# Decoder blocks on one core: GpSimd taken out of the splits, token mix shared with ACT, decay by exponentials, a sixth split slot

## The chip, the cores and the metric

One core of one Trainium2 chip runs one program. The metric is the device time of one execution in microseconds; lower is better. Engines are called as in the profile: PE is TensorE, DVE VectorE, ACT ScalarE, POOL GpSimd, SP the sync engine whose queue issues the DMAs.

## The reference

Two stacked models in float32 on 256 tokens of width 1024. The first block runs three mixers side by side (differential attention, an RWKV-7 recurrence, attention over 256 memory rows), projects them back, and runs a mixture of experts with 16 experts of which two are chosen per token. Then come four SwiGLU blocks (ffn0 to ffn3, inner width 2816), a hybrid attention layer (hyb) behind ffn0 and a sliding-window one (swa) behind ffn2. The change touches above all this part:

```python
cols = cols + (prev - cols) * mu
...
w = -jax.nn.softplus(-(w0 + jnp.tanh(xw) @ w2)) - 0.5
...
decay = jnp.exp(-jnp.exp(w))
...
state = (state * w_t[:, :, None, :]
         + sa[..., None] * (kk_t * a_t)[:, :, None, :]
         + v_t[..., None] * k_t[:, :, None, :])
```

## The kernel before

**Split products.** A float32 product is done as three matmuls of a faster type (`mm3`, lines 97 to 101): every operand is split into a high half (a cast by ACT, line 93) and a low half (operand minus high half, line 94), and high x high, low x high and high x low are added in PSUM. Weights arrive by SP in 2 MB tiles ("raw", `load`, line 85) and are split 1024 columns at a time into "wh" and "wl". These go round in slots: three of the pool wsp, and from the first ffn on two more of the pool lend (`weights`, line 168; NW = 3, NV = 2). A split waits until TensorE has done with the slot's last user. `self.lo` names the engine of line 94: DVE, except for seven of the eight tiles of the recurrence's input and the K projection of the differential attention, eleven splits in all, where it is POOL. The activations are split in `prep` (lines 116 to 137): eight transposes by TensorE for each half of the tokens, in two groups a = 0, 1; for each, DVE multiplies by the gain ("xf", line 133), ACT casts to "xh" (line 134), and "xl" is taken on POOL for a = 0 and on DVE for a = 1 (line 135). `prep` runs eight times: for x, for mem, and at each of the six block boundaries. The norm's "rstd" (lines 105, 106) is on POOL.

**Boundaries.** `project_back` does its last few k tiles (TAIL) for token half 0 and then for half 1. Behind each half the sum is added to h (lines 369, 371), and `prep` of the next block runs for that half while TensorE does the other.

**The front.** `mixers` interleaves one generator, `rwkv`, with the projections. `rwkv_inputs` (from line 640) makes eight tiles: a product, "cur" = product x norm (line 653), "shd" = previous token minus this one (line 655), "mix" = shd x mu + cur (line 656), all on DVE. `rwkv` takes the decay from a sigmoid by two tanh on ACT (lines 692, 693), then on DVE 1 - z, a reciprocal and 2z - 1 (lines 709 to 711), a running product over each chunk of 64 tokens by a scan with resets (line 712), and its reciprocal (line 715).

**The MoE.** Behind the logits, h is split once more, "hx" on ACT and "hy" on POOL (lines 1170, 1171), and multiplied with one-hot places to gather the tokens of each expert. The experts' weights (100 MB) pass through slots: wsp, lend, raw and "half" tiles.

**Order.** Every engine works through its queue in order. The queues' orders are made when the program is built, by the Tile scheduler from its own estimate of a timeline (`schedule_with_timeline_sim=True`); nothing is written out by hand but the order of `staggered` and of the generators.

Of the kernel before, what the change touches and what calls it, by code (L numbers as in the profile page):

```python
# [26 lines left out]
class Net:  # L27
    def __init__(self, ctx, tc, I):
        self.ctx, self.tc, self.nc, self.I = ctx, tc, tc.nc, I
        nc = self.nc  # L30
        self.const = ctx.enter_context(tc.tile_pool(name="const", bufs=1))
        self.wk = ctx.enter_context(tc.tile_pool(name="wk", bufs=2))
        self.dram = ctx.enter_context(tc.tile_pool(name="dram", bufs=1, space=DRAM))
        self.raw0 = ctx.enter_context(tc.tile_pool(name="raw0", bufs=RAW))
        self.base = [self.raw0] * RAW
        self.wsp = ctx.enter_context(tc.tile_pool(name="wsp", bufs=NW))
        self.lend = ctx.enter_context(tc.tile_pool(name="lend", bufs=NV))
        self.ahead, self.lo, self.nsc = [], nc.vector, 3
        self.n = 0
        self.setup()  # L40
# [23 lines left out]
    def setup(self):  # L64
        nc = self.nc
        self.ident = self.const.tile([128, 128], F32, name="ident")
        nc.gpsimd.memset(self.ident, 1.0)
        nc.gpsimd.affine_select(self.ident, self.ident, pattern=[[-1, 128]], compare_op=OP.is_equal,
                                fill=0.0, base=0, channel_multiplier=1)
        self.mhalf = self.const.tile([128, 1], F32, name="mhalf")  # L70
        nc.gpsimd.memset(self.mhalf, -0.5)
        self.cols = self.const.tile([128, NCOL], F32, name="cols")
        nc.scalar.dma_start(self.cols, self.I["cols"])

    def col(self, name, i=0, n=1):
# [12 lines left out]
    def split(self, x):  # L88
        nc = self.nc
        n = x.shape[-1]  # L90
        p = next(self.splits)
        hi, lo = (p.tile([128, 1024], F32, name=self.nm(z), tag=z).bitcast(F32R) for z in ("wh", "wl"))
        nc.scalar.copy(hi[:, :n], x)  # L93
        self.lo.tensor_tensor(lo[:, :n], x, hi[:, :n].bitcast(F32), OP.subtract)  # L94
        return hi, lo
# [20 lines left out]
    def prep(self, h, gain, into=None):  # L116
# [5 lines left out]
        def fill(t):  # L122
            for a in range(2):
                ps = self.trp()
                for i in range(4):
                    k = a * 4 + i
                    nc.tensor.transpose(ps[:, i * 128:(i + 1) * 128], h[t][:, k * 128:(k + 1) * 128], self.ident)  # L127
                p3 = ps.rearrange("p (k t) -> p k t", k=4)
                dh = xh[:, a * 4:a * 4 + 4, t * 128:(t + 1) * 128]
                dl = xl[:, a * 4:a * 4 + 4, t * 128:(t + 1) * 128]  # L130
                xf = self.wk.tile([128, 4, 128], F32, name=self.nm("xf"), tag="xf")
                g = self.col(gain, a * 4, 4)
                nc.vector.tensor_tensor(xf, p3, g.unsqueeze(2).to_broadcast([128, 4, 128]), OP.mult)
                nc.scalar.copy(dh, xf)  # L134
                (nc.vector if a else nc.gpsimd).tensor_tensor(dl, xf, dh.bitcast(F32), OP.subtract)  # L135
            rs[t] = self.rms(h[t], D, 1.0 / 32)
# [25 lines left out]
    def weights(self, extra, nsplit):  # L162

        with ExitStack() as st:
            pools = list(self.base)
            if extra:
                pools += [st.enter_context(self.tc.tile_pool(name=self.nm("raw"), bufs=extra))] * extra
            self.splits = itertools.cycle([self.wsp] * NW + [self.lend] * nsplit)
            self.ring = itertools.cycle(pools)
            yield  # L170
# [261 lines left out]
    def hyb(self, h, x, follow):  # L432
# [7 lines left out]
        ps = self.projN(self.by_k(self.load(self.I["hyb_c"]), 296), 0, 296, xh, xl, True)  # L440
        cw = self.natural(ps, self.pair(264, "cw0", "cw1"), rs)
        kiT = self.repeated_T([z[:, 264:296] for z in ps], rs, "kiT", 1)
# [101 lines left out]
    def mixers(self, x, more, follow):  # L544
# [19 lines left out]
        next(rwkv)  # L564
        self.lo = nc.gpsimd
        dist, nlam = self.diff_consts()
        k = project(W[3], 512, self.lent("wl"))
        self.lo = nc.vector
        next(rwkv)
# [43 lines left out]
        self.slots = [pools[c] for c in MOE_SLOTS]  # L613
        self.lo, self.nsc = nc.vector, 4
        return logits
# [23 lines left out]
    def rwkv_inputs(self, W, xh, xl, bc):  # L639
# [3 lines left out]
        for n, i in enumerate(RW_ORDER):  # L643
# [3 lines left out]
            elif n == 4:  # L647
                raw = self.load(W[1])
            self.lo = nc.gpsimd if n else nc.vector
            ps = self.projT(self.by_col(raw, n % 4), xh, xl)  # L650
            cur = self.sb([T + 1], "cur", cls="r")
            nc.gpsimd.memset(cur[:, 0:1], 0.0)
            nc.vector.tensor_tensor(cur[:, 1:], ps[:, :T], bc, OP.mult)  # L653
            d = self.sb([T], "shd", cls="r")
            nc.vector.tensor_sub(d, cur[:, :T], cur[:, 1:])
            nc.vector.scalar_tensor_tensor(out[i // 2][:, i % 2, :], d, self.k1("mu", i, 1), cur[:, 1:],
                                           OP.mult, OP.add)
        return out

    def rwkv(self, rw):  # L660
# [10 lines left out]
        vec.tensor_scalar(half[:, 0:6], self.k1("wa0k"), 0.5, None, OP.mult)  # L671
        dk = 0.25 * math.exp(-0.5)
        vec.memset(half[:, 6:7], -dk)
        vec.memset(half[:, 7:8], -0.5)
# [15 lines left out]
        for hp in range(2):  # L690
            S = sg[:, hp, :]
            act.activation(S, zp[:, hp * T:hp * T + T], AF.Tanh, bias=half[:, hp:hp + 1], scale=0.5)
            act.activation(S, S, AF.Tanh, scale=-dk, bias=half[:, 6:7])
        for hp in range(2):
# [10 lines left out]
        for hp in range(2):  # L705
            S = sg[:, hp, :]
            dec, wx = sb([4, 65], "dec"), sb([4, 65], "wx")
            pool.memset(dec[:, :, 0:1], 0.0)
            vec.tensor_scalar(S, S, -1.0, 1.0, OP.mult, OP.add)
            vec.reciprocal(S, S)  # L710
            vec.tensor_scalar(dec[:, :, 1:], c4(S), 2.0, -1.0, OP.mult, OP.add)
            vec.tensor_tensor_scan(wx.rearrange("p c t -> p (c t)"), dec.rearrange("p c t -> p (c t)"),
                                   self.k1("reset"), 0.0, OP.mult, OP.add)
            iw = sb([4, 64], "iw")
            vec.reciprocal(iw, wx[:, :, 1:])
            Wx.append(wx)
# [414 lines left out]
    def moe(self, h, x):  # L1131
# [37 lines left out]
        for t in range(2):  # L1169
            nc.scalar.copy(hx[t], h[t])  # L1170
            nc.gpsimd.tensor_tensor(hy[t], h[t], hx[t].bitcast(F32), OP.subtract)

# [262 lines left out]
    def front(self, h):  # L1435
# [4 lines left out]
        with ExitStack() as more:  # L1440
# [3 lines left out]
            with self.phase():  # L1444
                y = self.moe(h, x)
        ahead = [self.load(self.I["ffn0"][0], 2)]
        self.moe_overflow(h)
# [65 lines left out]
for _n, _w in (("mu", 8), ("wa0k", 6), ("kk_g", 2), ("rk_g", 2), ("bsel", 2), ("wa2", 256), ("g2", 256), ("gn_w", 256),  # L1513
               ("gn_b", 256), ("maskkr", 128), ("low8", 64), ("bd8", 64), ("eye", 64), ("off16", 64), ("off32", 64),
               ("off64", 64), ("reset", 260)):
    COLS1[_n] = (NC1, _w)
# [44 lines left out]
def cols1(X):  # L1561
# [28 lines left out]
    for b in (16, 32, 64):  # L1590
        put(f"off{b}", one((q // b == m // b) & (2 * q // b != 2 * m // b)))
    put("reset", one(np.arange(260) % 65 == 0))
    return c
# [94 lines left out]
```

## Time and profile before

| | |
|---|---|
| median of 3 runs | 1452.94 us (1452.23 to 1453.97) |
| the profiled execution | 1451.34 us |
| its span in the profile | 1449.6 us, mean PE clock 0.983 |
| busy: PE, PEld, DVE, ACT, POOL | 1383.6, 1042.0, 760.6, 605.6, 127.9 us |
| HBM traffic | 291 MB read, 202 GB/s over the span |

The span goes from the first to the last instruction; the execution's own time has something around it. A group gives the busy time of all instructions of a line, engine, operation and shape, the mean of one, and the idle time of their engine just before them with what ended it. "X <- Y" in the waits reads: X stood idle until Y was done. A timeline row is one instruction or several like it (x2), in brackets its engine's idle time before it. Where a helper records the line, one line stands for many places; the tile's name tells them apart.

### The profile page before, as it was taken

What the parts mean: (1) busy time and instruction counts of PE and PEld (TensorE: products, weight loads), DVE (VectorE), ACT (ScalarE), POOL (GpSimd) and SP (SyncE); (2) the same over time, 40 slices, a digit from 0 to 9 for tenths busy, and PEclk for the clock granted to TensorE, in tenths of its full rate; (3) what the DMA queues carried; (4) which work ended last, traced back from release to release, by engine and by line L of the source; (5) the groups of instructions that cost most, each with busy time, mean ns of one, the idle gap of its engine ahead of it and who ended that gap; (6) DMA issues with size and microseconds to landing.
All of it is one profiled execution on the core that took longest, in us unless ns stands there. A gap on an engine that the chain in (4) does not pass through costs nothing.

```text
span 1449.6 us, 18902 instructions
## 1 busy us (share of the span) xinstructions
PE 1383.6 (95%) x7650; PEld 1042.0 (72%) x7650; DVE 760.6 (52%) x1233; ACT 605.6 (42%) x951; POOL 127.9 (9%) x150
## 2 busy tenths in 40 slices
PE   7899989999998999999898999999999989999997
PEld 6687664344336888878677888878888877788886
DVE  6967651112125555456865555455555466555544
ACT  5345431111114444347454444344444456444442
POOL 6514110000001000010111000010000010100001
PEclk9999889999998999999999999999999999999999
DMA  7243379999965544355333544454444632365520
GB/s 305 90 183 139 145 319 368 419 409 419 420 285 213 194 174 175 130 216 194 126 117 139 210 174 174 153 225 175 175 174 160 240 129 111 131 214 182 185 88 29
DMA packets 35371, 293.81 MB, mean 203 GB/s; under 512 B 3728, under 2 KB 8112, under 8 KB 16080
## 3 DMA queue, kind: packets, MB, share of 16 engines
q1 hardware_dynamic: 29952, 286.58, 52.4%
q10 hardware_dynamic: 5328, 5.98, 1.2%
q8 instruction: 62, 1.02, 0.3%
q14 instruction: 29, 0.24, 0.0%
HBM read 291.45 MB, written 1.10 MB: 202 GB/s over the span
## 4 chain that ended last, share of the span: by engine, by line
PE 64%; DVE 2%; ACT 1%; POOL 1%; issue 1%; ACTq 0%; POOLq 0%; DVEq 0%
PE acc L101 20%; PE acc L99 20%; PE acc L100 19%; PE tr L206 1%; PE acc L322 1%; PE tr L318 1%; DVE wl L94 1%; POOL xl L135 1%; ACT wh L93 1%; PE acc L288 1%; PE acc L289 1%; PE acc L323 0%; ACT sq L113 0%; DVE h L371 0%; PE tr L127 0%
## 5 line engine op out<-in xcount | busy, mean ns | idle before, releaser
L94 DVE TENSOR_TENSOR wl<-raw,wh 128x1024 fp32r<-128x1024 f32 (+1 forms) x338 | 412.5, 1223 | 377.6 <-ACT wh L93 377.0
L93 ACT CAST wh<-raw 128x1024 fp32r<-128x1024 f32 (+1 forms) x349 | 363.4, 1045 | 412.8 <-PE acc L101 367.7
L101 PE MATMUL acc<-wh,xl 128*128 128x512 f32 (+2 forms) x896 | 336.0, 376 | 7.2 <-POOL xl L135 7.2
L99 PE MATMUL acc<-wh,xh 128*128 128x512 f32 (+2 forms) x896 | 337.2, 378 | 1.7 <-ACT xh L134 1.2
L100 PE MATMUL acc<-wl,xh 128*128 128x512 f32 (+2 forms) x896 | 335.2, 374 | 3.0 <-DVE wl L94 3.0
L101 PEld LDWEIGHTS acc<-wh,xl 128*128 128x128 f32 x896 | 169.5, 189 | 41.4 <-POOL xl L135 9.2
L100 PEld LDWEIGHTS acc<-wl,xh 128*128 128x128 f32 x896 | 169.8, 190 | 35.3 <-DVE wl L94 3.7
L99 PEld LDWEIGHTS acc<-wh,xh 128*128 128x128 f32 x896 | 169.8, 189 | 35.1 <-ACT xh L134 2.2
L101 PE MATMUL acc<-wh,hl 128*128 128x512 f32 x352 | 137.4, 390 | 0.0
L100 PE MATMUL acc<-wl,hh 128*128 128x512 f32 x352 | 137.2, 390 | 0.0
L99 PE MATMUL acc<-wh,hh 128*128 128x512 f32 x352 | 136.7, 389 | 0.0
L105 POOL TENSOR_SCALAR rstd<-ss 128x1 f32<-128x1 f32 x22 | 8.2, 371 | 940.8 <-ACT sq L113 938.9
L101 PEld LDWEIGHTS acc<-wh,hl 128*128 128x128 f32 x352 | 66.1, 188 | 13.6
L99 PEld LDWEIGHTS acc<-wh,hh 128*128 128x128 f32 x352 | 66.1, 188 | 13.6
L100 PEld LDWEIGHTS acc<-wl,hh 128*128 128x128 f32 x352 | 66.1, 188 | 13.5
L99 PE MATMUL acc<-xh,wh 128*128 128x256 f32 x224 | 65.8, 294 | 2.1 <-DVE cur L653 1.3
L100 PE MATMUL acc<-xl,wh 128*128 128x256 f32 x224 | 63.9, 286 | 1.8 <-POOL xl L135 1.0
L101 PE MATMUL acc<-xh,wl 128*128 128x256 f32 x224 | 64.2, 288 | 0.0
L1298 PE MATMUL acc<-half,xe 128*64 128x512 f32 x248 | 59.6, 596 | 0.0
L1331 DVE TENSOR_SCALAR yf<-tr,gate 128x512 f32<-128x512 f32 x16 | 12.0, 751 | 81.0 <-PE tr L1324 80.8
L99 PEld LDWEIGHTS acc<-xh,wh 128*128 128x128 f32 x224 | 43.4, 194 | 5.9 <-ACT wh L93 2.7
L100 PEld LDWEIGHTS acc<-xl,wh 128*128 128x128 f32 x224 | 43.1, 193 | 2.5 <-POOL xl L135 1.3
(458 smaller groups left out, 1748.7 us busy)
## 6 DMA issues: line engine op xcount, KB each, us to landing
raw<-in_ffn SPq DMA_DIRECT2D x63, 2048.0 KB, 8.0
half<-in_moe SPq DMA_DIRECT2D x45, 1024.0 KB, 12.9
raw<-in_moe SPq DMA_DIRECT2D x13, 2048.0 KB, 15.6
raw<-in_hyb SPq DMA_DIRECT2D x7, 2048.0 KB, 7.9
wl<-in_moe SPq DMA_DIRECT2D x23, 512.0 KB, 13.7
wh<-in_moe SPq DMA_DIRECT2D x23, 512.0 KB, 14.8
raw<-in_win SPq DMA_DIRECT2D x4, 2048.0 KB, 10.1
raw<-in_swa SPq DMA_DIRECT2D x4, 2048.0 KB, 8.7
```

The lines of the kernel that those rows point to most:

```text
L93: nc.scalar.copy(hi[:, :n], x)
L94: self.lo.tensor_tensor(lo[:, :n], x, hi[:, :n].bitcast(F32), OP.subtract)
L99: mm(out, a[0], b[0], start=start, stop=False)
L100: mm(out, a[0], b[1], start=False, stop=False)
L101: mm(out, a[1], b[0], start=False, stop=stop)
L135: (nc.vector if a else nc.gpsimd).tensor_tensor(dl, xf, dh.bitcast(F32), OP.subtract)
L206: nc.tensor.transpose(ps[:, i * 128:(i + 1) * 128], m[:, i * 128:(i + 1) * 128], self.ident)
L288: nc.tensor.matmul(ps[:, 0:128], qT[r, 0:128], kT[r, 0:128], start=True, stop=True)
L289: nc.tensor.matmul(ps[:, 128:384], qT[r, 128:256], kT[r, :], start=True, stop=True)
L318: nc.tensor.transpose(pt[:, i * 128:(i + 1) * 128], s2[e][:, i * 128:(i + 1) * 128], self.ident)
L322: nc.tensor.matmul(po[r, :T], v[0][:, c:c + 64], pT[:, :T], start=True, stop=False)
L1298: last = mm(ps[c][e * 64:e * 64 + 64, :], xe[:, k, o + e * 64:o + e * 64 + 64], w[i][e][:, c * 512:c * 512 + 512], start=k == 0, stop=k == 7)
```

## The change

Seven things. (1) `self.lo` goes: the low half of every split is on DVE. So are "xl" for a = 0 in `prep` and "hy" in the MoE (there in four pieces of 512 columns). (2) The token mix is written as cur x (1 - mu), on ACT with a scale per partition, plus previous x mu, on DVE; a tile "keep" holds 1 - mu. (3) The decay: one tanh on ACT, + 1 on DVE, a running sum by a scan that restarts at each chunk (constant "keep" for "reset"), and two exponentials on ACT for the running product and its reciprocal. (4) `weights` opens a pool "spare" of one more slot wherever it adds lend's: six slots instead of five from ffn0 on. (5) `room` puts two unused tiles of 16 words, one in the pool of constants and one in wk. (6) A pair of tiles in hyb is 320 columns wide instead of 264. (7) The DMA scratch is 512 instead of 1024. The diff, without most of its context:

```diff
@@ -35,7 +35,7 @@
         self.lend = ctx.enter_context(tc.tile_pool(name="lend", bufs=NV))
-        self.ahead, self.lo, self.nsc = [], nc.vector, 3
+        self.ahead, self.nsc = [], 3
         self.n = 0
@@ -69,8 +69,14 @@
         nc.gpsimd.memset(self.mhalf, -0.5)
+        self.room(self.const, 16)
         self.cols = self.const.tile([128, NCOL], F32, name="cols")
         nc.scalar.dma_start(self.cols, self.I["cols"])
+
+    def room(self, pool, words):
+
+        z = pool.tile([128, words], F32, name=self.nm("room"), tag=f"room{words}", bufs=1)
+        self.nc.gpsimd.memset(z, 0.0)
@@ -91,7 +97,7 @@
         nc.scalar.copy(hi[:, :n], x)
-        self.lo.tensor_tensor(lo[:, :n], x, hi[:, :n].bitcast(F32), OP.subtract)
+        nc.vector.tensor_tensor(lo[:, :n], x, hi[:, :n].bitcast(F32), OP.subtract)
         return hi, lo
@@ -132,7 +138,7 @@
                 nc.scalar.copy(dh, xf)
-                (nc.vector if a else nc.gpsimd).tensor_tensor(dl, xf, dh.bitcast(F32), OP.subtract)
+                nc.vector.tensor_tensor(dl, xf, dh.bitcast(F32), OP.subtract)
             rs[t] = self.rms(h[t], D, 1.0 / 32)
@@ -165,7 +171,8 @@
                 pools += [st.enter_context(self.tc.tile_pool(name=self.nm("raw"), bufs=extra))] * extra
-            self.splits = itertools.cycle([self.wsp] * NW + [self.lend] * nsplit)
+            spare = [st.enter_context(self.tc.tile_pool(name=self.nm("spare"), bufs=1))] if nsplit else []
+            self.splits = itertools.cycle([self.wsp] * NW + [self.lend] * nsplit + spare)
             self.ring = itertools.cycle(pools)
@@ -438,7 +445,7 @@
         ps = self.projN(self.by_k(self.load(self.I["hyb_c"]), 296), 0, 296, xh, xl, True)
-        cw = self.natural(ps, self.pair(264, "cw0", "cw1"), rs)
+        cw = self.natural(ps, [z[:, :264] for z in self.pair(320, "cw0", "cw1")], rs)
         kiT = self.repeated_T([z[:, 264:296] for z in ps], rs, "kiT", 1)
@@ -562,10 +569,8 @@
         next(rwkv)
-        self.lo = nc.gpsimd
         dist, nlam = self.diff_consts()
         k = project(W[3], 512, self.lent("wl"))
-        self.lo = nc.vector
         next(rwkv)
@@ -611,7 +616,7 @@
         self.slots = [pools[c] for c in MOE_SLOTS]
-        self.lo, self.nsc = nc.vector, 4
+        self.nsc = 4
         return logits
@@ -646,14 +651,16 @@
                 raw = self.load(W[1])
-            self.lo = nc.gpsimd if n else nc.vector
             ps = self.projT(self.by_col(raw, n % 4), xh, xl)
...
             nc.vector.tensor_tensor(cur[:, 1:], ps[:, :T], bc, OP.mult)
+            if n == 0:
+                keep = self.sb([8], "keep", cls="r")
+                nc.vector.tensor_scalar(keep, self.k1("mu"), -1.0, 1.0, OP.mult, OP.add)
             d = self.sb([T], "shd", cls="r")
-            nc.vector.tensor_sub(d, cur[:, :T], cur[:, 1:])
-            nc.vector.scalar_tensor_tensor(out[i // 2][:, i % 2, :], d, self.k1("mu", i, 1), cur[:, 1:],
+            nc.scalar.activation(d, cur[:, 1:], AF.Copy, scale=keep[:, i:i + 1])
+            nc.vector.scalar_tensor_tensor(out[i // 2][:, i % 2, :], cur[:, :T], self.k1("mu", i, 1), d,
                                            OP.mult, OP.add)
@@ -669,8 +676,7 @@
         vec.tensor_scalar(half[:, 0:6], self.k1("wa0k"), 0.5, None, OP.mult)
-        dk = 0.25 * math.exp(-0.5)
-        vec.memset(half[:, 6:7], -dk)
+        dk = 0.5 * math.exp(-0.5)
         vec.memset(half[:, 7:8], -0.5)
@@ -690,7 +696,6 @@
             act.activation(S, zp[:, hp * T:hp * T + T], AF.Tanh, bias=half[:, hp:hp + 1], scale=0.5)
-            act.activation(S, S, AF.Tanh, scale=-dk, bias=half[:, 6:7])
         for hp in range(2):
@@ -706,13 +711,12 @@
             pool.memset(dec[:, :, 0:1], 0.0)
-            vec.tensor_scalar(S, S, -1.0, 1.0, OP.mult, OP.add)
-            vec.reciprocal(S, S)
-            vec.tensor_scalar(dec[:, :, 1:], c4(S), 2.0, -1.0, OP.mult, OP.add)
-            vec.tensor_tensor_scan(wx.rearrange("p c t -> p (c t)"), dec.rearrange("p c t -> p (c t)"),
-                                   self.k1("reset"), 0.0, OP.mult, OP.add)
+            vec.tensor_scalar(dec[:, :, 1:], c4(S), 1.0, None, OP.add)
+            vec.tensor_tensor_scan(wx.rearrange("p c t -> p (c t)"), self.k1("keep"),
+                                   dec.rearrange("p c t -> p (c t)"), 0.0, OP.mult, OP.add)
             iw = sb([4, 64], "iw")
-            vec.reciprocal(iw, wx[:, :, 1:])
+            act.activation(iw, wx[:, :, 1:], AF.Exp, scale=dk)
+            act.activation(wx, wx, AF.Exp, scale=-dk)
             Wx.append(wx)
@@ -1168,7 +1172,8 @@
             nc.scalar.copy(hx[t], h[t])
-            nc.gpsimd.tensor_tensor(hy[t], h[t], hx[t].bitcast(F32), OP.subtract)
+            for s in (slice(0, 512), slice(512, 1024)):
+                tt(hy[t][:, s], h[t][:, s], hx[t][:, s].bitcast(F32), OP.subtract)
@@ -1443,6 +1448,7 @@
                 y = self.moe(h, x)
+        self.room(self.wk, 16)
         ahead = [self.load(self.I["ffn0"][0], 2)]
@@ -1512,7 +1518,7 @@
                ("gn_b", 256), ("maskkr", 128), ("low8", 64), ("bd8", 64), ("eye", 64), ("off16", 64), ("off32", 64),
-               ("off64", 64), ("reset", 260)):
+               ("off64", 64), ("keep", 260)):
     COLS1[_n] = (NC1, _w)
@@ -1589,7 +1595,7 @@
         put(f"off{b}", one((q // b == m // b) & (2 * q // b != 2 * m // b)))
-    put("reset", one(np.arange(260) % 65 == 0))
+    put("keep", one(np.arange(260) % 65 != 0))
     return c
@@ -1677,7 +1683,7 @@
     arrays = {k: np.ascontiguousarray(v) for k, v in pack(inputs).items()}
-    nc = _bacc.Bacc("TRN2", target_bir_lowering=False, num_devices=1, dynamic_dma_scratch_size=1024)
+    nc = _bacc.Bacc("TRN2", target_bir_lowering=False, num_devices=1, dynamic_dma_scratch_size=512)
     I = {k: nc.dram_tensor(f"in_{k}", list(v.shape), mybir.dt.from_np(v.dtype), kind="ExternalInput").ap()
```

## Rows read from the trace of the kernel before

**Rows 1.** The page's busy times (part 1) and the chain that ended last (part 4).

```profile
PE 1383.6 (95%) x7650; PEld 1042.0 (72%) x7650; DVE 760.6 (52%) x1233; ACT 605.6 (42%) x951; POOL 127.9 (9%) x150
...
PE acc L101 20%; PE acc L99 20%; PE acc L100 19%; PE tr L206 1%; PE acc L322 1%; PE tr L318 1%; DVE wl L94 1%; POOL xl L135 1%; ACT wh L93 1%; PE acc L288 1%; PE acc L289 1%; PE acc L323 0%; ACT sq L113 0%; DVE h L371 0%; PE tr L127 0%
```

**Rows 2.** Whom TensorE waited for, whole span: total us, times, longest us.

```profile
PE tr L127 <- DVE xf L133: 7.8, 6, 2.4
...
PE acc L101 <- POOL xl L135: 7.2, 5, 2.2
...
PE acc L100 <- DVE wl L94: 3.0, 2, 2.4
...
PE acc L100 <- POOL xl L135: 1.0, 1, 1.0
```

**Rows 3.** Stretches: length, busy us of PE, PEld, DVE, ACT, POOL, PE clock, DMA, GB/s.

```profile
20.00:72.00 52.00, 44.44 (x309) 37.19 (x308) 48.17 (x66) 23.75 (x38) 29.87 (x25) 1.00 0.37 141
...
217.40:253.70 36.30, 36.30 (x185) 16.44 (x181) 4.85 (x13) 5.91 (x11) 0.00 (x0) 1.00 0.92 368
...
1164.50:1171.30 6.80, 5.73 (x27) 5.73 (x28) 4.05 (x4) 1.78 (x4) 2.30 (x2) 0.52 0.02 9
```

**Rows 4.** Groups of POOL: busy us, mean ns of one, idle before and its releaser.

```profile
L94 POOL TENSOR_TENSOR wl<-raw,wh 128x1024 fp32r<-128x1024 f32 x11 | 27.0, 2463 | 7.9 <-ACT wh L93 7.8
...
L135 POOL TENSOR_TENSOR xl<-xf,xh 128x512 fp32r<-128x512 f32 x14 | 21.0, 1505 | 15.1 <-ACT xh L134 15.1
...
L1171 POOL TENSOR_TENSOR hy<-h,hx 128x1024 fp32r<-128x1024 f32 x2 | 4.7, 2364 | 0.1
```

**Rows 5.** Groups of DVE, shapes apart.

```profile
L94 DVE TENSOR_TENSOR wl<-raw,wh 128x1024 fp32r<-128x1024 f32 x333 | 407.7, 1227 | 374.2 <-ACT wh L93 373.6 <-DVEq L1359 0.2
...
L656 DVE SCALAR_TENSOR_TENSOR mix<-shd,c,cur 128x256 f32<-128x256 f32 x8 | 9.7, 1217 | 0.2
...
L655 DVE TENSOR_TENSOR shd<-cur 128x256 f32<-128x256 f32 x8 | 9.5, 1187 | 0.6
...
L715 DVE RECIPROCAL iw<-wx 128x256 f32<-128x256 f32 x2 | 3.5, 1740 | 0.0
```

**Rows 6.** Timeline of the front: start, us, engine and step.

```profile
22.10 2.62 POOL L94 TENSOR_TENSOR wl<-raw,wh 128x1024 fp32r<-128x1024 f32 x1 [3.43 <-ACT wh L93]
...
22.88 2.11 DVE L655 TENSOR_TENSOR shd<-cur 128x256 f32<-128x256 f32 x1
...
25.95 0.42 DVE L655 TENSOR_TENSOR shd<-cur 128x256 f32<-128x256 f32 x1
```

**Rows 7.** Timeline of the boundary from hyb to ffn1.

```profile
773.77 1.22 DVE L94 TENSOR_TENSOR wl<-raw,wh 128x1024 fp32r<-128x1024 f32 x1
...
774.65 0.42 POOL L105 TENSOR_SCALAR rstd<-ss 128x1 f32<-128x1 f32 x1 [30.72 <-ACT sq L113]
...
776.24 1.25 PE L127 MATMUL tr<-ident,h 128*128 128x128 f32 x8 [1.54 <-DVE xf L133]
...
776.70 1.22 DVE L94 TENSOR_TENSOR wl<-raw,wh 128x1024 fp32r<-128x1024 f32 x1
...
776.92 1.08 POOL L105 TENSOR_SCALAR rstd<-ss 128x1 f32<-128x1 f32 x1 [1.20 <-ACT sq L113]
...
777.90 0.69 DVE L135 TENSOR_TENSOR xl<-xf,xh 128x512 fp32r<-128x512 f32 x1
```

**Rows 8.** Timeline of TensorE in the front, two steps behind an idle stretch.

```profile
36.91 0.35 PE L99 MATMUL acc<-xh,wh 128*128 128x256 f32 x1 [1.25 <-DVE cur L653]
...
56.71 1.26 PE L127 MATMUL tr<-ident,mem 128*128 128x128 f32 x8 [2.37 <-DVE xf L133]
```

**Rows 9.** Whom SP's DMA queue waited for, 0 to 80 us.

```profile
SPq L576 <- POOL cur L652: 14.3, 1, 14.3
```

**Rows 10.** Group of ACT in the recurrence.

```profile
L696 ACT ACTIVATE lent<-mix,c 128x256 f32<-128x256 f32 x2 | 1.0, 498 | 0.0
```

**Rows 11.** Timeline of DVE ahead of the MoE.

```profile
207.06 0.17 DVE L1229 COPY G<-rstd 128x8 f32<-128x8 f32 x1 [1.95 <-POOL rstd L106]
```

## The prediction

> **What bounds the kernel now.** I read the page's busy times and its chain first, then whom TensorE waited for, then its idle stretches in order of time with the other engines beside them. TensorE is busy 1383.6 of 1449.6 us, and the chain that ended last runs three fifths through the three matmul lines of the split product [rows 1]. So the kernel is bound by matmul work that the change doesn't touch. What an edit can win is the remaining 66.0 us of idle TensorE, and the stretches where its clock is at the lower level. The list of waits says who ends that idle time [rows 2]: "xf" on DVE 7.8 us, "xl" on POOL 7.2 and 1.0, the split's low half "wl" on DVE 3.0. The diff touches every one of these. It doesn't touch the wait behind the top-k mask in the hyb layer, nor the routing.
>
> Two places hold these waits. **The front** (20 to 72 us): DVE is busy 48.2 of 52.0 us, POOL 29.9, TensorE 44.4 [rows 3]. **The six block boundaries** (MoE to ffn0, and the five after it), where the next block's input is normalised, transposed and split while TensorE drains the last block.
>
> **Why DVE is full in the front.** POOL takes 2.46 us for a 128x1024 low half, DVE 1.22 [rows 4, 5]. While POOL does one, short DVE steps get long: the subtraction of the token mix takes 0.42 us at 25.95, but at 22.88 it takes 2.11 and ends at 24.99, as POOL's split, begun at 22.10, ends at 24.72 [rows 6]. Over the eight tiles the two mix steps cost 9.5 + 9.7 us [rows 5]; at 0.45 each, an estimate from the short one, they would cost 7.2, so some 12 us of DVE's front are this waiting. Reciprocals of 1.7 us, two for each head pair, stand in the same queue [rows 5].
>
> **The change part by part.**
>
> *Splits to DVE, front.* DVE gets 11 splits x 1.22 = 13.4 us, and four "xl" of 0.69 (attn and mem) = 2.8 [rows 5, 7]. It loses the 12 us of waiting, the eight subtractions (3.4 at 0.42), and by the decay edit four reciprocals (the two of L715 take 3.5 [rows 5], the others the same: 7). Sum: 16.2 in, about 22.4 out, so DVE's load falls by some 6 us instead of growing. TensorE's idle time there that DVE ends is 1.25 ("cur", at 36.91), 2.37 ("xf" of mem, at 56.71) [rows 8] and both waits on "wl", 3.0 [rows 2]: 6.6 us. I take **-5.5**; the rest stays because chains through DVE are still there. Bounds: -6.6, and +2 if splits queue behind each other (one and a half of them). The load of mem waited 14.3 us on SP's queue for a step of POOL's queue [rows 9], with the next weight load behind it; with the splits gone from POOL it goes out earlier, and moves with this term.
>
> *Token mix on ACT, decay by exponentials.* ACT gets eight scaled copies and four exponentials and loses two tanh, all of 256 columns, where the scaled copy that is there takes 0.50 us [rows 10]: 10 x 0.50 = +5.0 us on an engine busy 23.8 of 52.0 us [rows 3]. Taken at **0**; what hides it is TensorE's own 44 us there. If that cover were gone, one copy would be late by one high half in ACT's queue, about 1 us, on the last tile: bounds -0.5 and +1. Behind a late copy on DVE wait the mix and what follows it. The recurrence's chain loses two reciprocals and one step; what that wins is in the first term, whose last two waits stand beside it.
>
> *"xl" to DVE at the boundaries.* Here 12 of the 16 low halves leave POOL (1.51 us mean, waiting included [rows 4]) for DVE at 0.69 [rows 7], in order behind what DVE has. TensorE's waits ended by "xl" are 7.2 + 1.0 = 8.2 us, the 1.0 at the very start [rows 2]. A step that takes 0.69 for 1.51 would save 8.2 x 0.54 = 4.4; where two halves ran on both engines at once they lengthened each other, which goes too. Against it, a split (1.22) may stand in front of it. I take **-5**; bounds -8.2 and 0. Behind the new step are the "h" additions and splits, 0.69 later each; TensorE needs those only after the first k tiles.
>
> *Sixth slot.* One more slot lets one split of the next block run before the boundary. At hyb to ffn1 a split of 1.22 us stands on DVE at 773.77, in front of the addition and of "xf", for which TensorE then waits 1.54 [rows 7]. Waits on "xf" outside the front are 7.8 - 2.37 = 5.4 us [rows 2, 8]. I take **-3**, half a split at each of five; bounds -5.4 and 0. Inside a block it brings nothing, as no wait on "wl" but the front's two is in the list.
>
> *MoE "hy" to DVE.* POOL's two steps of 2.36 us [rows 4] go; DVE gets four of 0.69 (2.8 us). DVE idles 1.95 us there, waiting for a POOL "rstd" [rows 11], which covers most of it, and the logits' matmuls end no sooner: **0**, bounds -0.5 and +1.4.
>
> *Padding tiles, smaller DMA scratch, wider pair:* two memsets of 16 words, and other addresses. No row shows a time that hangs on an address: **0**, bounds -1 and +1.
>
> Sum: -5.5 - 5 - 3 = **-13.5 us**. The profiled execution took 1451.34 us, 1.7 more than its span; the median of the runs, 1452.94, is 1.6 above it. So 1437.8 for such an execution, **1439.4** against the median.
>
> One thing speaks against the change: POOL keeps the "rstd" steps, and more of DVE's work now stands beside them. At 776.92 such a step takes 1.08 us and ends at 778.00, beside a DVE split that runs from 776.70 to 777.92 [rows 7]. I add nothing for it, since the next user of "rstd" is the eviction behind all k tiles. The Trainium skill (SBUF — State Buffer, "Who interferes with whom") says that a DVE instruction with two SBUF inputs and a GpSimd one that reads SBUF shut each other out for their whole length, whichever issues first; this row agrees, and by the rule every split or "xl" moved to DVE can hold an "rstd" (a rival, below).
>
> **Rivals.**
> - *The MoE's weights eat the front's gain.* The DMA share is 0.92 at 368 GB/s in the MoE's first stretch [rows 3]; if the weights land no sooner, a TensorE that starts earlier waits. Only the boundaries count then: -8, **1445**. Against: TensorE is busy 36.3 of 36.3 us there, and the loads start on slots that the front frees.
> - *All bounds, and a clock drop with them.* -6.6 - 8.2 - 5.4, and the 6.8 us at clock 0.52 from 1164.5 [rows 3], the lower level, just behind TensorE's waits at ffn2 to swa: worth 3.3. Together -23.5: **1429**.
> - *"rstd" on POOL is late.* Lengthened from the 0.42 at 774.65 to the 1.08 at 776.92 [rows 7], at six boundaries and on the path: +4.0, **1443.4**. Against: nothing in the waits of TensorE names "rstd".
> - *Slower: DVE is the new bound.* If DVE's long steps in the front came from something else than POOL, DVE would get 16.2 us and lose 10.4: +5.8 us on an engine 93% full [rows 3], all of it on TensorE; and at five boundaries "xl" would stand behind a split, 1.22 + 0.69 against 1.51, +0.4 each. About +8: **1461**. It decides where DVE has no idle time left between 20 and 72 us. Against: the lengthened steps end with POOL's [rows 6].
> - *It doesn't do what it says:* the order on the queues is made anew, and DVE's freed time falls where TensorE doesn't wait. 0 to -2: **1452**.
>
> **Chances.** Forecast 0.56 (its own range 1433 to 1447), all bounds 0.13, DMA 0.11, "rstd" 0.05, no gain 0.07, slower 0.08. A measurement here tells about 0.2% (2.9 us) from no change. Faster by more than that: the first four, less a little of the forecast's own bounds: 0.84. Within: the fifth, 0.07. Slower: 0.09. The range runs from 1427 (all bounds, and 2 for the unknown small ones) to 1450 (short of the fifth case) and leaves out some two in ten.
>
> **What would show it.** Right: no POOL row for L94, L135 or L1171; the mix steps at 0.42 to 0.5 us; DVE under 85% busy between 20 and 72 us; the wait of L101 on "xl" under 3 us in total; the MoE's gathers 5 us sooner; a DVE split fewer between the "h" addition and "xf" at the boundaries. Wrong: DVE over 95% busy in the front, TensorE's waits on "xl" or "wl" as large as before, or new table loads on ACT in the recurrence.

## The result, and the profile after

| | before | after |
|---|---|---|
| median of 4 runs | 1453.03 us (1452.23 to 1453.97) | 1429.70 us (1428.48 to 1431.53) |
| the profiled execution, its span | 1451.34, 1449.6 us | 1430.63, 1428.9 us |
| TensorE busy / idle in the span | 1383.6 / 66.0 us | 1378.0 / 50.9 us |
| mean granted clock | 0.983 | 0.979 |

The ratio is 0.9842, 95% interval [0.9829, 0.9854]: 23.3 us faster, where 13.5 were forecast; 1429.7 lies in the range of the forecast (1427 to 1450), near its lower end. Of the 20.7 us by which the span is shorter, 15.1 are idle time of TensorE and 5.6 busy time. The forecast counted on idle time alone.

Busy times and chain of the page, which answer to [rows 1]:

```profile
PE 1378.0 (96%) x7650; PEld 1051.2 (74%) x7650; DVE 747.7 (52%) x1250; ACT 610.0 (43%) x961; POOL 77.5 (5%) x123
...
PE acc L105 20%; PE acc L107 20%; PE acc L106 20%; PE tr L213 1%; PE acc L329 1%; DVE wl L100 1%; PE tr L325 1%; PE acc L296 1%; PE acc L295 1%; PE acc L330 0%; ACT sq L119 0%; DVE h L376 0%; DVE h L378 0%; DVE xf L139 0%; ACT wh L99 0%
```

Whom TensorE waited for, against [rows 2]: the waits on GpSimd's "xl" and those on "wl" are gone, and 2.1 us of waits on "xl" from DVE are left. The wait on "xf" is 5.6 instead of 7.8. One entry is new: "ka", behind the top-k mask in hyb, 3.7 us, where the kernel before waited 6.3 us for the mask itself, "madd".

```profile
PE tr L133 <- DVE xf L139: 5.6, 5, 1.6
...
PE acc L295 <- DVE ka L386: 3.7, 2, 3.2
...
PE acc L107 <- DVE xl L141: 1.5, 2, 0.8
...
PE acc L106 <- DVE xl L141: 0.6, 1, 0.6
```

The front, as a stretch (columns as in [rows 3]), and two groups of DVE there, against [rows 5]: DVE is busy 42.1 of 52 us instead of 48.2, TensorE 50.9 instead of 44.4 (418 matmuls instead of 309), and the mix step takes 478 ns instead of 1217.

```profile
20.00:72.00 52.00, 50.89 (x418) 43.81 (x417) 42.12 (x81) 30.89 (x52) 6.25 (x14) 1.00 0.38 146
...
L100 DVE TENSOR_TENSOR wl<-raw,wh 128x1024 fp32r<-128x1024 f32 x14 | 17.1, 1220 | 5.2 <-ACT wh L99 5.2
L663 DVE SCALAR_TENSOR_TENSOR mix<-cur,c,shd 128x256 f32<-128x256 f32 x8 | 3.8, 478 | 0.3 <-POOL cur L656 0.3
```

The same 52 us hold more work now. Up to 6.5 us behind the first gather of the MoE, where both kernels have done the same 1709 matmuls, TensorE's idle time falls from 25.7 to 16.3 us and DVE's busy time from 155.7 to 141.1. Before, then after, columns as in [rows 3]:

```profile
0.00:217.40 217.40, 191.71 (x1709) 153.96 (x1711) 155.71 (x327) 96.30 (x195) 79.13 (x86) 0.95 0.51 197
```

```profile
0.00:206.90 206.90, 190.56 (x1709) 156.58 (x1711) 141.07 (x332) 100.12 (x205) 44.90 (x71) 0.94 0.53 207
```

The MoE's gathers, a tile's summary (first and last start): before, then after. The first starts 10.5 us sooner and the last 10.4, so the lead stays unchanged through the MoE.

```profile
L1189 PE MATMUL tr<-P,hx x64: 274/283/553, 210.9 to 370.7; 128*128 128x256 f32 x64
```

```profile
L1194 PE MATMUL tr<-P,hx x64: 278/283/553, 200.4 to 360.3; 128*128 128x256 f32 x64
```

Behind the MoE the lead was followed from matmul to matmul, each against the one of the same tile and number in the other trace. It is 10.5 us at the end of the MoE, 8.3 at the start of ffn0, 10.5 at its end, 12.1 in hyb, 13.2 and 15.6 at the start and end of ffn1, 15.3 and 17.6 of ffn2, 17.7 at the end of swa, 18.4 and 20.6 at the start and end of ffn3. Within each ffn it grows at an even pace over the first 120 us, by 2.7 us, gives back some 0.4 and then stands still. Boundaries do not look like that. The two rows below show a stretch of 80 us in the up half of ffn1, in which TensorE is busy throughout at the upper clock: 357 matmuls before, 370 after.

```profile
796.00:876.00 80.00, 80.00 (x357) 64.76 (x356) 43.15 (x42) 36.15 (x40) 0.00 (x0) 1.00 0.53 193
```

```profile
783.00:863.00 80.00, 80.00 (x370) 66.47 (x369) 44.81 (x44) 38.38 (x43) 0.00 (x0) 1.00 0.55 198
```

The timeline of TensorE in ffn0 shows why, before and after: nine matmuls take 2.10 us, and 2.04. From start to start the median over the kernel is 233 ns before and 227 after, in all three matmuls of a split product whose stationary operand is xh or xl. In the down half, with hh and hl, it is 227 or 226 in both kernels. (The up half of an ffn multiplies the normalised input xh, xl by the first weights, the down half the inner activations hh, hl by the last.)

```profile
500.15 0.39 PE L100 MATMUL acc<-wl,xh 128*128 128x512 f32 x1
...
502.25 0.39 PE L100 MATMUL acc<-wl,xh 128*128 128x512 f32 x1
```

```profile
490.87 0.39 PE L106 MATMUL acc<-wl,xh 128*128 128x512 f32 x1
...
492.91 0.39 PE L106 MATMUL acc<-wl,xh 128*128 128x512 f32 x1
```

The last weights of each up half are taken with 256 moving columns, and there it is the other way round. Nine matmuls take 1.02 us before and 1.08 after, 113 ns and 120 from start to start, which is what the lead gives back:

```profile
573.02 0.28 PE L99 MATMUL acc<-wh,xh 128*128 128x256 f32 x1
...
574.04 0.28 PE L99 MATMUL acc<-wh,xh 128*128 128x256 f32 x1
```

```profile
562.03 0.28 PE L105 MATMUL acc<-wh,xh 128*128 128x256 f32 x1
...
563.11 0.28 PE L105 MATMUL acc<-wh,xh 128*128 128x256 f32 x1
```

So the lead grows by 2.2 to 2.4 us in each ffn, by 9.1 in the four.

And the clock: at two levels, full and half, a mean of 0.983 is half clock in 2 x 0.017 x 1449.6 = 49 us, one of 0.979 in 60 us. Between MoE and ffn0 the lower level lasts longer (columns as in [rows 3], before and then after), which is where the lead fell from 10.5 to 8.3.

```profile
444.00:455.00 11.00, 8.14 (x27) 6.38 (x28) 9.79 (x13) 4.33 (x8) 3.24 (x6) 0.53 0.74 279
```

```profile
434.00:448.00 14.00, 10.60 (x32) 7.91 (x33) 11.64 (x17) 5.51 (x9) 2.50 (x4) 0.51 0.81 317
```

### The profile page after: what moved, and what is told of

It reads as the page before. It is cut to its first block, busy times and chain, and to the rows that moved or that the text cites. A ratio compares the mean times of both kernels' runs of the same rounds, so it can differ in the third digit from the quotient of the medians.

```text
span 1428.9 us, 18895 instructions
## 1 busy us (share of the span) xinstructions
PE 1378.0 (96%) x7650; PEld 1051.2 (74%) x7650; DVE 747.7 (52%) x1250; ACT 610.0 (43%) x961; POOL 77.5 (5%) x123
## 3 DMA queue, kind: packets, MB, share of 16 engines
q8 instruction: 62, 1.02, 0.3%
## 4 chain that ended last, share of the span: by engine, by line
PE 65%; DVE 3%; ACT 1%; issue 1%; ACTq 0%; POOLq 0%; POOL 0%
PE acc L105 20%; PE acc L107 20%; PE acc L106 20%; PE tr L213 1%; PE acc L329 1%; DVE wl L100 1%; PE tr L325 1%; PE acc L296 1%; PE acc L295 1%; PE acc L330 0%; ACT sq L119 0%; DVE h L376 0%; DVE h L378 0%; DVE xf L139 0%; ACT wh L99 0%
## 5 line engine op out<-in xcount | busy, mean ns | idle before, releaser
L100 DVE TENSOR_TENSOR wl<-raw,wh 128x1024 fp32r<-128x1024 f32 (+1 forms) x349 | 426.1, 1224 | 377.0 <-ACT wh L99 374.9
L105 PE MATMUL acc<-wh,xh 128*128 128x512 f32 (+1 forms) x896 | 334.5, 375 | 2.4 <-ACT xh L140 1.8
L106 PE MATMUL acc<-wl,xh 128*128 128x512 f32 (+1 forms) x896 | 333.1, 372 | 0.0
L105 PEld LDWEIGHTS acc<-wh,hh 128*128 128x128 f32 x352 | 66.1, 188 | 13.5
```

Of the source, the lines that this page charges most:

```text
L100: nc.vector.tensor_tensor(lo[:, :n], x, hi[:, :n].bitcast(F32), OP.subtract)
L105: mm(out, a[0], b[0], start=start, stop=False)
L106: mm(out, a[0], b[1], start=False, stop=False)
```

## Experiments

Each kernel is named by its label. The kernel before ran beside each of them; its medians there were 1451.68 to 1453.68 us.

| kernel | us | ratio to before, 95% interval | TensorE idle, us | spacing with xh, ns |
|---|---|---|---|---|
| before_pads | 1446.31 | 0.9951 [0.9932, 0.9970] | 64.1 | 227 |
| after_nopads | 1441.43 | 0.9928 [0.9912, 0.9945] | 53.6 | 233 |
| after_noc | 1428.10 | 0.9830 [0.9813, 0.9846] | 51.5 | 227 |
| after_now | 1438.04 | 0.9901 [0.9885, 0.9918] | 51.8 | 233 |
| slots5_off128 | 1435.66 | 0.9885 [0.9869, 0.9902] | 52.8 | 232 |
| before_lodve | 1445.93 | 0.9941 [0.9919, 0.9964] | 59.2 | |
| before_mixdec | 1448.26 | 0.9971 [0.9960, 0.9982] | 61.0 | |
| before_front | 1449.00 | 0.9973 [0.9957, 0.9990] | 65.5 | |
| before_front_xl2 | 1439.25 | 0.9907 [0.9892, 0.9922] | 53.8 | |
| after_xlpool | 1439.10 | 0.9909 [0.9892, 0.9925] | 60.4 | |
| after_xlbound | 1429.77 | 0.9837 [0.9823, 0.9850] | 52.4 | |
| after_5slots | 1426.23 | 0.9820 [0.9806, 0.9833] | 51.1 | |

Idle is span less TensorE's busy time, from the page; the spacing is the median from start to start of acc<-wh,xh with 512 columns.

### The addresses

**before_pads**: the kernel before with the change's addresses.

```diff
+        self.room(self.const, 16)
...
+        self.room(self.wk, 16)
...
-        cw = self.natural(ps, self.pair(264, "cw0", "cw1"), rs)
+        cw = self.natural(ps, [z[:, :264] for z in self.pair(320, "cw0", "cw1")], rs)
...
-dynamic_dma_scratch_size=1024
+dynamic_dma_scratch_size=512
```

> The kernel before with the addresses of the change alone: the two unused tiles of 16 words, the DMA scratch of 512 and the pair of 320 columns. Every queue keeps its order; only the two memsets come in. xh and xl move from 448 to 0, wh and wl from 384 to 0 (byte address in the partition, modulo 512). Theory P (the address decides how fast the matmuls of the up half of an ffn follow each other, 233 ns before and 227 after): the spacing of acc<-wh,xh falls to 227 ns, the time by 9 to 12 us, to about 1442. Rival Q (the spacing comes from another part of the change, the sixth slot or GpSimd's absence): spacing stays 233 ns, time within 1 us of before.

Spacing 227: the addresses alone do it. The time fell by 7 us by the ratio and 5.4 by the medians, less than Theory P gave. In its trace the lead grows by 9.3 us in the four ffns, as in the changed kernel (9.1), and shrinks between them, where the mean clock, 0.976, tells of more half clock than the 0.983 of before. In the stretch of the up half shown above for the kernel before it has 366 matmuls for 357:

```profile
796.00:876.00 80.00, 80.00 (x366) 66.37 (x366) 44.85 (x44) 37.50 (x42) 0.00 (x0) 1.00 0.56 197
```

**after_nopads**: the same edit taken back from the changed kernel.

> The changed kernel without the two unused tiles, with the scratch of 1024 and the pair of 264 again: addresses modulo 512 as in the kernel before, all else changed. Theory P: spacing of acc<-wh,xh back at 233 ns, time 9 to 12 us above the changed kernel, about 1440. Rival Q: spacing 227 ns, time within 1 us of 1429.7.

Spacing 233, and 1441.43: by the ratios 0.9928 - 0.9842 = 0.0086, or 12.5 us, 11.7 by the medians. Theory P holds, Rival Q falls. In its trace the lead stands still within every ffn, and the stretch of the up half has 360 matmuls:

```profile
786.00:866.00 80.00, 80.00 (x360) 64.53 (x359) 44.61 (x43) 37.41 (x41) 0.00 (x0) 1.00 0.54 192
```

The two pairs of kernels, 7 and 12.5 us, lie on either side of the 9 us that the traces show within the ffns. What is left over is of the size by which the clock moves the time of one kernel (last section).

**after_noc, after_now**: the changed kernel with one of the two unused tiles gone, which tells whose start counts.

```diff
-        self.room(self.const, 16)
```

> The changed kernel without the unused tile in the pool of constants: xh, wh and hh all start at 448 modulo 512, so stationary and moving operand have the same offset. If the stationary operand's own start decides (64 off a multiple of 128): 233 ns in the up half and also in the down half, where both kernels had 227; time 15 us above the changed kernel. If the difference between the two operands' starts decides: 227 ns everywhere, time within 1 us of 1429.7.

```diff
-        self.room(self.wk, 16)
```

> The changed kernel without the unused tile in wk: xh starts at 0, wh and hh at 448 modulo 512. If the stationary operand's own start decides: 227 ns in the up half (xh at 0), 233 in the down half (hh at 448), time 6 us above the changed kernel. If the difference between the two starts decides: 233 in the up half, 227 in the down half, time 9 to 12 above. If the moving operand's start decides: 233 in both, 15 above.

Without the first tile all of them start at 448 and nothing is lost: spacing 227 in both halves, 1428.10. Without the second xh starts at 0 and wh at 448, the up half is back at 233 and the down half, where hh starts at 448 like wh, stays at 227; the time is 8.6 us above the changed kernel by the ratios. So it is not the stationary operand's own start, nor the moving one's, but whether the two start alike. The rows are 80 us of the up half in after_noc, then in after_now.

```profile
783.00:863.00 80.00, 80.00 (x368) 66.34 (x367) 44.92 (x44) 37.53 (x41) 0.00 (x0) 1.00 0.56 205
```

```profile
790.00:870.00 80.00, 80.00 (x362) 64.79 (x361) 44.30 (x44) 37.01 (x43) 0.00 (x0) 1.00 0.52 184
```

**slots5_off128**: a start 128 bytes apart, with five slots.

```diff
-        self.room(self.wk, 16)
+        self.room(self.wk, 48)
...
-            self.splits = itertools.cycle([self.wsp] * NW + [self.lend] * nsplit + spare)
+            self.splits = itertools.cycle([self.wsp] * NW + [self.lend] * nsplit)
```

> The changed kernel with five split slots (as in after_5slots) and an unused tile of 48 words instead of 16 in wk: xh starts at 0, wh and wl at 128 modulo 512, hh and wh still have the same start. Theory D (only the difference of the two starts modulo 128 counts): acc<-wh,xh stays at 227 ns, time 1425 to 1428, a second sample of the five slots with every queue in the same order. Rival E (any difference of the two starts costs): 233 ns, time 8 to 11 us above after_5slots, about 1436.

Theory D falls: 232 ns, and 9.4 us above after_5slots, which has the same order on every queue. The row is the same stretch of the up half, with 362 matmuls again.

```profile
786.00:866.00 80.00, 80.00 (x362) 65.05 (x361) 43.76 (x44) 37.10 (x42) 0.00 (x0) 1.00 0.52 184
```

### The front

**before_lodve** and **before_mixdec** do the two halves of the front's edits alone, **before_front** both.

```diff
-        self.lo.tensor_tensor(lo[:, :n], x, hi[:, :n].bitcast(F32), OP.subtract)
+        nc.vector.tensor_tensor(lo[:, :n], x, hi[:, :n].bitcast(F32), OP.subtract)
```

> The kernel before with the low half of all splits on DVE and nothing else changed. Theory L (the waiting of DVE beside GpSimd's splits was the cost): DVE gets 13.4 us and loses 12 of waiting, mix steps at 0.45 us, the gathers 5 to 7 us sooner. Rival M (the new token mix and decay, which take some 10 us off DVE, carry the gain): the gathers no sooner than before or up to 2 us later.

> The kernel before with the new token mix and the new decay alone; GpSimd keeps its splits. Theory L: the mix step that is left on DVE is still lengthened by GpSimd's splits (over 1 us), the gathers 2 to 4 us sooner. Rival M: 7 us sooner or more.

The mechanism of Theory L is shown by a group each of DVE in the front, first of before_lodve, then of before_mixdec: with GpSimd's splits gone the mix step takes 467 ns; with them it takes 1246, new mix or old.

```profile
L656 DVE SCALAR_TENSOR_TENSOR mix<-shd,c,cur 128x256 f32<-128x256 f32 x8 | 3.7, 467 | 0.0
```

```profile
L659 DVE SCALAR_TENSOR_TENSOR mix<-cur,c,shd 128x256 f32<-128x256 f32 x8 | 9.9, 1246 | 3.2 <-ACT shd L658 3.2
```

The lead over before is 5.1 us from 72 to 160 us in before_lodve, as Theory L has it, and 2.0 in before_mixdec. By the gathers it is 3.1 and -0.2, short of the 5 to 7 and 2 to 4 that Theory L gave: more half clock between 156 and 216 us takes the difference. Neither half alone makes the 10.5 us.

> The kernel before with the front's edits alone: the low half of all splits on DVE, the token mix shared with ACT, the decay by exponentials. xl, hy, slots and addresses stay. Theory F (the front's edits win the whole 10.5 us by which the MoE starts sooner in the changed kernel, and nothing else): TensorE reaches the MoE's gathers 10 us sooner, time 1441 to 1443. Rival G (part of it is the xl of the first blocks, now on DVE too): gathers 6 to 8 us sooner, time 1445 to 1447.

By the median, 1449.0 us, both fell. The trace is that of a run of 1453.16 us; four of the ten runs took 1445.0 to 1446.0, which is Rival G's time, and of those there is no trace. In the trace the lead is some 10 us at 72 us, still 9 to 10 at 138, and -1.3 at the gathers. It is lost between 138 and 180 us: TensorE runs at the lower clock from 138 us on, behind two short waits and through a run of 64x64 matmuls of the recurrence, and then waits twice for an "xf" of the differential attention. A stretch of before_front, and two of TensorE's waits there:

```profile
138.00:156.00 18.00, 16.90 (x185) 13.83 (x186) 7.28 (x31) 5.81 (x18) 0.77 (x1) 0.53 0.00 1
```

```profile
PE tr L1091 <- DVE xf L1054: 6.4, 2, 3.3
PE tr L1029 <- DVE sc L1022: 2.0, 2, 1.1
```

**after_xlpool**: one line of the change taken back.

```diff
-                nc.vector.tensor_tensor(dl, xf, dh.bitcast(F32), OP.subtract)
+                (nc.vector if a else nc.gpsimd).tensor_tensor(dl, xf, dh.bitcast(F32), OP.subtract)
```

> The changed kernel with the first of each two xl on GpSimd again. Theory X (moving xl was worth little, as idle time that goes at a boundary is partly handed back): time 1 to 3 us above the changed kernel. Rival Y (the 5 us of the prediction were won, and a lower clock elsewhere hides them): 4 to 7 us above, with waits on GpSimd's xl of 7 us in all. No gain at all, or a loss by moving it: within 1 us or below.

9.4 us above the changed kernel, more than any theory gave, and 8.9 of it are there at the gathers already: the same loss at the same place, with half clock from 139 us on and the same wait on "xf" (6.3 us). The queues differ. Up to the MoE, TensorE has the same order of instructions in after_xlpool as in before_front, and another one in the changed kernel, in which the recurrence's chain and the attention's heads alternate otherwise, nearly as in the kernel before.

**before_front_xl2** and **after_xlbound** tell the front's "xl", with the order that it brings, from the boundaries' "xl": in both the "xl" of x and mem is on DVE and that of the six boundaries on GpSimd (the first is before_front, the second the changed kernel).

```diff
+        front = self.preps < 2
+        self.preps += 1
...
-                (nc.vector if a else nc.gpsimd).tensor_tensor(dl, xf, dh.bitcast(F32), OP.subtract)
+                (nc.vector if a or front else nc.gpsimd).tensor_tensor(dl, xf, dh.bitcast(F32), OP.subtract)
```

> The kernel with the front's edits alone (as in before_front), and besides the first of the two xl on DVE for x and mem; at the six boundaries it stays on GpSimd. TensorE's queue up to the MoE then has exactly the order of the changed kernel; with GpSimd's xl in the front it has another one. Theory O (the order that the planner makes decides whether the front's gain is kept behind 100 us): the gathers 9 to 11 us sooner than before, the half clock begins behind 150 and not at 138 us, time 1441 to 1444, 5 to 8 below before_front. Rival N (what was lost behind 100 us in before_front comes from the xl itself, two or three steps of 1.5 us on GpSimd): 1 to 3 us below before_front, order or not.

1439.25, 9.75 us below before_front's median: more than Theory O gave, and still some 6 below its four shortest runs. The gathers are 9.3 us sooner, and the clock stays at its upper level until 152 us:

```profile
138.00:152.00 14.00, 11.35 (x157) 8.57 (x155) 11.74 (x44) 7.77 (x24) 4.50 (x8) 1.00 0.01 3
152.00:163.00 11.00, 9.81 (x29) 6.01 (x28) 7.84 (x23) 5.32 (x16) 0.67 (x1) 0.53 0.55 206
```

Another 3.9 us come in hyb, by order as well: in the kernel before, "qa" and "ka" stand on DVE behind most of the top-k steps, and TensorE waits 6.3 us; here they stand between them, and the wait there is 1.8. Rival N falls: the last of the front's four "xl" on GpSimd ends at 68 us in before_front, and some 10 us of lead outlast it until 138. Theory O fits, with one thing open: in both pairs of kernels the order changes together with the engine of that "xl", and no kernel has the one without the other. Which of the orders the planner makes was not steered by hand; whether the new mix and decay are needed for the good one, beside the splits, was not tried.

### The boundaries

> The changed kernel with the first of the two xl on GpSimd at the six boundaries alone; x and mem keep theirs on DVE, so the front keeps the order of the changed kernel. Theory O: nearly all of the 9.4 us between after_xlpool and the changed kernel was the front's order; what is left for the boundaries is 0 to 3 us: time 1429 to 1433. Rival Y (the 5 us of the prediction): 1434 to 1437.

1429.77, beside the changed kernel's 1429.70: at the boundaries the move of "xl" is worth nothing that the runs tell from 0. GpSimd's "xl" is waited for again, as before the change:

```profile
PE acc L108 <- POOL xl L144: 5.7, 5, 2.2
PE tr L136 <- DVE xf L142: 5.6, 5, 1.6
...
PE acc L298 <- DVE ka L389: 2.6, 3, 1.8
```

Yet all idle time together is only 1.5 us more (52.4 for 50.9). With "xl" on DVE other waits are longer, "ka" 3.7 for 2.6, "xh" 2.3 for 1.9, "qT" 1.4 for 1.0.

**after_5slots**:

```diff
-            self.splits = itertools.cycle([self.wsp] * NW + [self.lend] * nsplit + spare)
+            self.splits = itertools.cycle([self.wsp] * NW + [self.lend] * nsplit)
```

> The changed kernel with five split slots instead of six. Theory S (the prediction's 3 us): 2 to 5 us above the changed kernel, one more split of 1.22 us in front of xf at a boundary. Rival Z (a split that runs ahead of the boundary was hidden anyway, or the idle time it frees comes back as half clock): within 1.5 us of the changed kernel.

Theory S falls with the wrong sign: 1426.23, faster than the changed kernel. Idle time is the same (51.1 for 50.9), and so is the wait that the sixth slot was to remove. At hyb to ffn1 the same split stands on DVE between the addition to h and "xf", with six slots (first fence) and with five (second):

```profile
761.32 1.22 DVE L100 TENSOR_TENSOR wl<-raw,wh 128x1024 fp32r<-128x1024 f32 x1
...
763.79 1.25 PE L133 MATMUL tr<-ident,h 128*128 128x128 f32 x8 [1.62 <-DVE xf L139]
```

```profile
755.97 1.22 DVE L100 TENSOR_TENSOR wl<-raw,wh 128x1024 fp32r<-128x1024 f32 x1
...
758.44 1.26 PE L133 MATMUL tr<-ident,h 128*128 128x128 f32 x8 [1.62 <-DVE xf L139]
```

What differs is the clock: 0.985 in this trace and 0.979 to 0.985 in its runs, against 0.977 to 0.980 in the changed kernel's. In hyb TensorE waits 3.2 us for "ka" in both. Behind that wait the clock drops with six slots (first row), and with five it doesn't (second):

```profile
686.00:694.00 8.00, 6.68 (x35) 5.36 (x36) 6.71 (x32) 2.24 (x9) 0.00 (x0) 0.57 0.53 170
```

```profile
683.00:691.00 8.00, 6.69 (x58) 6.09 (x59) 7.93 (x39) 3.18 (x10) 0.33 (x1) 1.00 0.01 2
```

After_5slots is the fastest kernel of the study. Its runs (1424.62 to 1427.91) all lie below those of the changed kernel (1428.48 to 1431.53), but not beside them on one chip, and the two intervals against before touch. Beside it ran after_xlbound, also with six slots: 1427.69 to 1430.10. That it is faster by 3 us is likely, not settled. That the slot itself causes the clock's drops is not shown.

## Why the time lay in the range and the sum did not hold

The forecast's mechanism was idle time of TensorE in the front and at the boundaries, -13.5 us; the measured -23.3 has other parts. By pairs of kernels: the front with the order it brings -13.5 (before_front_xl2, 3.9 of it in hyb), addresses -7 to -12.5 (before_pads, after_nopads), "xl" at the boundaries 0 (after_xlbound), the sixth slot +3.2 (after_5slots, likely the clock's). In the trace the lead of 20.6 us at the end is 10.5 in front of the MoE, 9.1 in the four ffns by the addresses, 1.6 in hyb and 1.6 at the other boundaries, less the 2.2 that the clock takes between MoE and ffn0.

That 1429.7 lies in the range is in part luck. The lower end of the range stands for the case of all bounds, whose parts at the boundaries and of the clock did not come. Some 9 us came from a term put at 0; in the rest a front worth about twice its term made up for "xl" and slot, of whose 8 us the runs show nothing.

- **Splits to DVE, front: -5.5 forecast.** 9.3 to 10.5 us at the gathers, outside the bound of -6.6. The bound added up only the waits that DVE and "wl" end, 6.6 us; TensorE's idle time up to the gathers fell by 9.4. The reason given was right: the mix steps went to 0.48 us, and DVE's load fell instead of growing, by 14.6 us up to the gathers where "some 6" was forecast. The rule cited from the Trainium skill (SBUF — State Buffer, "Who interferes with whom") agrees with before_lodve, where only GpSimd's splits went and the mix step fell from 1217 to 467 ns. What the step left out is the order: the same front with another order of queues, before_front, keeps 4 us of it by the median, and none at the gathers of its trace.
- **Token mix and decay, 0.** In the sum they were cover for the first term, and that is how they work: 2.0 us of lead alone, and some 10 with the splits where the splits alone give 5.1. No table load of ACT came in (six in both kernels).
- **"xl" at the boundaries, -5.** The waits on "xl" went from 8.2 to 2.1 us as forecast ("under 3"), and the time did not move: 0, the end of the bound. The step that failed is to take a wait that is removed for time that is won.
- **Sixth slot, -3.** No idle time less, +3.2 us by the ratios. The split in front of "xf" stayed, the one sign of being right that did not come: a slot was not what it waited for.
- **MoE, 0.** Right: the lead is 10.5 us at both ends.
- **Padding, 0 within 1.** The step that failed most: some 9 us. "No row shows a time that hangs on an address" was wrong. The kernel before had two groups of the same shape, engine and operation with different means: acc<-wh,hh 389 ns in ffn0's down half (first row), acc<-wh,xh 396 in its up half (second). Six to seven nanoseconds in each of the 1920 matmuls of 512 columns in the four up halves (10 weight tiles x 2 token halves x 8 k x 3 products in each) are some 12 us, of which the 384 matmuls of 256 columns give back 2.5. In the memory map of the compiled program hh and wh start at 384 modulo 512, xh at 448.

```profile
L99 PE MATMUL acc<-wh,hh 128*128 128x512 f32 x52 | 20.2, 389 | 0.0
...
L99 PE MATMUL acc<-wh,xh 128*128 128x512 f32 x111 | 44.0, 396 | 0.0
```

- **Rivals.** The weights of the MoE didn't eat the front's gain. DVE was not the new bound: 81% busy in the front. The "rstd" steps did get longer, in the mean from 371 to 422 ns and from 644 to 681, but no wait of a matmul names "rstd". The case of all bounds lies at the measured 1429, but its own parts, the boundaries and the clock behind ffn2, did not happen: the lower level is still there, at 1147 and 1161 us. The last rival named the order made anew, for a gain of 0 to 2 us; the changed kernel and after_xlpool, which differ in one line and in the order that came with it, lie 9.4 us apart.

## What to carry to other kernels

Where two groups of one shape have different means in a busy stretch, ask what differs in their operands before looking for idle time: a few nanoseconds in thousands of matmuls came to some 9 us here, more than any one entry in the list of waits. Where a planner orders the queues, an edit is worth what the order made with it is worth; compare the queues' orders first, and measure an edit with the order held fixed. A wait that disappears from the list is not yet time won: compare the idle time in total and the clock.

## What the runs showed of the hardware that was not expected

A matmul with 512 moving columns follows the last one after 226 or 227 ns when the stationary operand's tile and the moving operand's start alike modulo 512 bytes in the partition (0 and 0, 448 and 448, 384 and 384), after 233 when they start 64 bytes apart (448 and 384, 0 and 448), and after 232 when they start 128 apart (0 and 128). With 256 moving columns it is the other way round: 113 ns at 64 apart and 120 at 0 and at 128 with xh stationary, with the last weights of the up halves, and 118 and 120 with xh moving, in the front. Other differences were not tried, and why it is so stays open.

The lower clock level depends on more than idle time. The changed kernel and after_5slots have 50.9 and 51.1 us of it, and mean clocks of 0.979 and 0.985; behind the same wait of 3.2 us in hyb the clock drops in one and not in the other. Nor does the level hold still from run to run: of ten runs of before_front four took 1452.7 to 1453.7 us with a mean clock of 0.975 or 0.976, four 1445.0 to 1446.0 with 0.980, and two lay between. It is the same program, and so a gain or loss of some 3 us of one kernel here can be the clock's alone.
